# Split weights of the first layer: stored to device memory when first made, loaded by later token chunks

## The chip, the cores and the metric

The kernel runs on one core of one Trainium2 chip. The metric is device time in microseconds, the median of several executions. A core has five engines with an instruction stream each: PE (matrix products; its weight loads are listed as PEld), DVE (elementwise work), ACT (elementwise work with lookup functions), POOL (elementwise work, here mostly for splitting numbers and for rotary embedding) and SP, whose instructions here issue transfers. Each engine takes its instructions in the order in which they stand and waits where one needs a result from another engine.

## The reference

Two layers of a hybrid decoder with 1024 channels, over 16 learned meta tokens and 2048 input tokens (2064 rows). The first layer is what the change touches:

```
def swa_conv_mixer(h, pos, w_in, sinks, conv_w, conv_b, ln_g, ln_b, w_pw2, w_out):
    q, k, v, g_a, glu_in, g_b = _split(h @ w_in, AB_SPLITS)
    q, k = apply_rope(q, pos), apply_rope(k, pos)
    a = sliding_window_sink_attention(q, k, v, sinks) * silu(g_a)
    u = glu_in[..., :512] * sigmoid(glu_in[..., 512:])
    c = silu(layer_norm(causal_depthwise_conv(u, conv_w, conv_b), ln_g, ln_b))
    c = (c @ w_pw2) * silu(g_b)
    return concatenate([a, c], axis=-1) @ w_out
h = h + rms_norm(swa_conv_mixer(rms_norm(h, ...), ...), ...)
```

`w_in` is 1024 x 2816, `w_pw2` 512 x 512, the convolution has 31 taps. The second layer is stick-breaking attention with its own projections. Everything is float32.

## The kernel before

**Split numbers.** A matrix product in float32 accuracy is made of three products of rounded numbers (type float32r): a number x is split into a high part (x rounded) and a low part (x minus the high part), and `mm3` (L126 to L130) adds high x high, high x low and low x high into one PSUM bank. In the rows of the profile, `hTh` and `hTl` are the high and low parts of the normed input, `wh` and `wl` those of a weight block.

**Weights.** `weights` (L112 to L121) brings one block of 128 x 8 x 128 float32 (512 KB): SP loads it into `raw` (L118), ACT rounds it into `wh` (L119), POOL subtracts it into `wl` (L120). `raw`, `wh` and `wl` have two buffers each for the input projection. L118 is given a priority 60 places earlier than its place in the program, so that loads run ahead.

**Stages of the first layer.** The tokens are worked on in four chunks: 528 tokens (chunk 0, in two pieces of 272 and 256) and three of 512. `stage1` does the input projection of a chunk: 22 blocks of `w_in`, each by a call of `proj` (L277 to L287): one `weights`, then 24 matmuls of 512 columns (48 narrower ones in chunk 0), then a follow-up on ACT or DVE. The order is: two halves of the gated unit (`glu_b`, `glu_a`), key, value, queries, and eight gate blocks (`gate`, L360 to L370), whose results are stored by L369 (`gad`, `gbd`). Block `glu_a` also puts a convolution of 31 taps per channel group into a list; a tap is one DVE instruction over the chunk (L294), and `run_bg` gives out six of them after each projection. `rope` shuffles halves by four small transfers (L334) and does its arithmetic on DVE and POOL (L338 to L343).

`stage2` does the rest for a chunk, in 128-token blocks: sliding-window attention (`swa`: scores on PE L429, masking and maximum on DVE L430, exponentials on ACT L441, products L470) and the convolution branch (`cbranch`: layer norm, activation, and the second product in `pw` with `w_pw2`, two weight blocks per call by the same `weights`, once for each of eight groups of blocks). Stage 2 of a chunk is interleaved with stage 1 of the next, one step at a time, so both run at once from chunk 1 on. After chunk 3 come its stage 2, interleaved with the output projection (`po`), and then layer 1.

**What sets the order.** The program is written with tile pools, and a scheduler orders each engine's instructions from their dependencies, priorities and buffer turns. All transfers are issued by SP in one order.

So each of the 22 blocks of `w_in` is loaded, rounded and subtracted four times, once per chunk, and each of the two blocks of `w_pw2` eight times: 104 calls of `weights` in all.

Of the kernel before, what the change touches and what calls it, by code (L numbers as in the profile page):

```python
# [11 lines left out]
F32R = mybir.dt.float32r  # L12
# [6 lines left out]
P = 128  # L19
D = 1024  # L20
KB = D // P
# [16 lines left out]
WP = 60  # L38
# [14 lines left out]
def tok0(t):  # L53
    return 0 if t == 0 else NM + (t - 1) * P


def toks(t):
    return NM if t == 0 else P
# [20 lines left out]
class Trunk:  # L79
# [29 lines left out]
        self.nc.gpsimd.tensor_scalar(hi, src, 1.0, 0.0, ALU.mult, ALU.add)  # L109
        self.nc.vector.tensor_tensor(lo, src, hi, ALU.subtract)  # L110

    def weights(self, pool, src, rpool, tag):  # L112
        nc = self.nc
        raw = rpool.tile([P, KB, P], F32, tag=tag, name="raw", bufs=2 if tag == "raw" else 1)
        wh = pool.tile([P, KB, P], F32R, tag="wh", name="wh")
        wl = pool.tile([P, KB, P], F32R, tag="wl", name="wl")
        with self.tc.high_priority(offset=WP):
            self.wdma = nc.sync.dma_start(raw, src).ins  # L118
        nc.scalar.copy(wh, raw)  # L119
        nc.gpsimd.tensor_tensor(wl, raw, wh, ALU.subtract)  # L120
        return wh, wl  # L121

    def mv(self, out, src):
# [54 lines left out]
    def layer0(self, after=None):  # L178
        tc, nc, a = self.tc, self.nc, self.a
        HALO = CW - 1  # L180
        qd = self.dram("q0d", [P, 2, 4, T], F32R)
        kd = self.dram("k0d", [2, 2, HD, T], F32R)
# [6 lines left out]
        c0, w2, w3 = (self.pool(left, n, b, side="left") for n, b in (("c0", 1), ("w2", 2), ("w3", 3)))  # L189
# [5 lines left out]
        pww = self.pool(left, "pww", 2, side="left")  # L195
# [3 lines left out]
        s1c, s1, s3 = (self.pool(early, n, b, side="right") for n, b in (("s1c", 1), ("s1", 2), ("s3", 2)))  # L199
# [51 lines left out]
        def stage1(c):  # L251
# [23 lines left out]
            steps.append((0.0, start))  # L275

            def proj(m, evac):  # L277
                wh, wl = self.weights(pww, a["w_in0"][m], s1, "raw")
                turns = late[:]
                late.clear()  # L280
                for s0, sn in subs:
                    ps = self.bank(next(banks), "pj")
                    for k in range(KB):
                        self.mm3(ps[:, :sn], wh[:, k], wl[:, k], st["h"][:, k, s0 : s0 + sn], st["l"][:, k, s0 : s0 + sn], k == 0, k == KB - 1)
                    evac(ps[:, :sn], s0, sn)
                for f in turns:
                    f()  # L287
# [12 lines left out]
            def glu_b(j):  # L300
                sg = s1.tile([P, 528], F32, tag="sg", name="sg")
                st["sg"] = sg
                proj(14 + j, lambda ps, s0, sn: nc.scalar.activation(sg[:, s0 : s0 + sn], ps, AF.Sigmoid))
                run_bg(CB)

            def glu_a(j):
                sg = st["sg"]
                u = s1.tile([P, HALO + 528], F32, tag="u", name="u")
                y = s1.tile([P, 528], F32, tag="y", name="y")
                nc.gpsimd.tensor_scalar(u[:, :HALO], uh[:, j], 1.0, 0.0, ALU.mult, ALU.add)  # L310
                proj(10 + j, lambda ps, s0, sn: nc.vector.tensor_tensor(u[:, HALO + s0 : HALO + s0 + sn], ps, sg[:, s0 : s0 + sn], ALU.mult))
                nc.gpsimd.tensor_scalar(uh[:, j], u[:, TC : TC + HALO], 1.0, 0.0, ALU.mult, ALU.add)
                conv(j, u, y)
                run_bg(CB)
# [14 lines left out]
            def rope(m, put):  # L329
                qr = s1.tile([P, 528], F32, tag="qr", name="qr", bufs=3)  # L330
                qs = s1.tile([P, 528], F32, tag="qs", name="qs")
                proj(m, lambda ps, s0, sn: nc.scalar.copy(qr[:, s0 : s0 + sn], ps))
                for b in range(4):
                    nc.sync.dma_start(qs[b * 32 : b * 32 + 32, :TC], qr[(b ^ 1) * 32 : (b ^ 1) * 32 + 32, :TC])  # L334
                run_bg(CB)

                def turn():
                    nc.vector.tensor_tensor(qr[:, :TC], qr[:, :TC], st["ctab"][:, :TC], ALU.mult)  # L338
                    nc.gpsimd.tensor_tensor(qs[:, :TC], qs[:, :TC], st["stab"][:, :TC], ALU.mult)
                    nc.vector.tensor_tensor(qr[:, :TC], qr[:, :TC], qs[:, :TC], ALU.add)  # L340
                    hi, lo = qs[:, :TC].bitcast(F32R), qr[:, :TC].bitcast(F32R)
                    nc.gpsimd.tensor_scalar(hi, qr[:, :TC], 1.0, 0.0, ALU.mult, ALU.add)
                    nc.gpsimd.tensor_tensor(lo, qr[:, :TC], hi, ALU.subtract)  # L343
                    put(qs, qr)

                late.append(turn)
# [132 lines left out]
        def cbranch(ut):  # L479
            b0 = tok0(ut[0])  # L480
            N = sum(toks(t) for t in ut)
            S = {}

            def stats():
                yl = w2.tile([P, 4, 272], F32, tag="yl", name="yl", bufs=1)
                nc.sync.dma_start(yl[:, :, :N], yd[:, :, b0 : b0 + N].rearrange("r p t -> p r t"))
                mv = w2.tile([P, 3, 2], F32, tag="mv", name="mv")
                nc.vector.memset(mv, 1.0)
                S["yns"] = yns = []
                for i, t in enumerate(ut):  # L490
                    n, o = toks(t), tok0(t) - b0
                    pt = self.bank("pt", "pt_y")
                    for j in range(4):
                        nc.tensor.transpose(pt[:n, j * P : j * P + P], yl[:, j, o : o + n], self.ident)
                    st = w2.tile([P, 6], F32, tag="bst", name="bst")
                    nc.vector.bn_stats(st[:n], pt[:n])
                    nc.vector.bn_aggr(mv[:n, i], st[:n])
                    yn = w3.tile([P, 512], F32, tag="yn", name="yn")
                    nc.scalar.copy(yn[:n], pt[:n])
                    yns.append(yn)  # L500
                cr = w2.tile([P, 3], F32, tag="cr", name="cr")
                self.rsqrt(w2, cr, mv[:, :, 1], 1.0, LEPS, 3, nc.gpsimd)
                for i, t in enumerate(ut):
                    n = toks(t)
                    nc.vector.tensor_scalar(yns[i][:n], yns[i][:n], mv[:n, i, 0:1], cr[:n, i : i + 1], ALU.subtract, ALU.mult)

            def act():
                yns = S["yns"]
                S["ch"] = ch = w2.tile([P, 4, 272], F32R, tag="ch", name="ch", bufs=1)
                S["cl"] = cl = w2.tile([P, 4, 272], F32R, tag="cl", name="cl", bufs=1)  # L510
                for j in range(4):
                    pt = self.bank("pt", "pt_c")
                    for i, t in enumerate(ut):
                        n, o = toks(t), tok0(t) - b0
                        nc.tensor.transpose(pt[:, o : o + n], yns[i][:n, j * P : j * P + P], self.ident[:n, :n])
                    sg = w2.tile([P, 272], F32, tag="csg", name="csg")
                    tt = w2.tile([P, 272], F32, tag="ctt", name="ctt")
                    nc.scalar.activation(sg[:, :N], pt[:, :N], AF.Sigmoid, bias=cv[:, 2, j : j + 1], scale=cv[:, 1, j : j + 1])
                    nc.scalar.activation(tt[:, :N], pt[:, :N], AF.Identity, bias=cv[:, 2, j : j + 1], scale=cv[:, 1, j : j + 1])
                    nc.vector.tensor_tensor(tt[:, :N], tt[:, :N], sg[:, :N], ALU.mult)  # L520
                    nc.scalar.copy(ch[:, j, :N], tt[:, :N])
                    nc.vector.tensor_tensor(cl[:, j, :N], tt[:, :N], ch[:, j, :N], ALU.subtract)

            def pw():
                ch, cl = S["ch"], S["cl"]
                gb = w2.tile([P, 4, 272], F32, tag="gb", name="gb", bufs=1)
                nc.sync.dma_start(gb[:, :, :N], gbd[:, :, b0 : b0 + N].rearrange("r p t -> p r t"))
                for m in range(4):
                    if m % 2 == 0:
                        wh, wl = self.weights(pww, a["w_pw2"][m // 2], w2, "yl")  # L530
                    ps = self.bank("pj", "pw")
                    for k in range(4):
                        kk = 4 * (m % 2) + k
                        self.mm3(ps[:, :N], wh[:, kk], wl[:, kk], ch[:, k, :N], cl[:, k, :N], k == 0, k == 3)
                    tt = w2.tile([P, 272], F32, tag="ctt", name="mc")
                    nc.vector.tensor_tensor(tt[:, :N], ps[:, :N], gb[:, m, :N], ALU.mult)
                    nc.sync.dma_start(md[4 + m, :, b0 : b0 + N], tt[:, :N])

            return stats, act, pw
# [580 lines left out]
```

## Time and profile before

| | |
|---|---|
| median of three executions | 2995.03 us (2994.13 to 2998.02) |
| the profiled execution, its own time | 2996.4 us |
| its span, first to last instruction | 2994.7 us |
| PE, DVE, ACT, POOL busy | 92%, 79%, 51%, 50% |
| L120 `wl` on POOL, whole span | 104 instructions, 273.4 us |
| L119 `wh` on ACT, until 1000 us | 102 instructions, 106.9 us |
| L294 taps on DVE, whole span | 480 instructions, 515.4 us |
| moved by DMA | 395.77 MB, of which 270.21 MB read from and 116.97 MB written to device memory |

The profile is of one execution. A row of a group gives line, engine, operation, output and inputs, shape and count, then busy time and the mean of one, then the engine's idle time before it and whose result ended it. A row of waits reads "who <- for whom: total us, times, longest". Matmuls overlap, and their shown lengths are modelled; the distance from one start to the next tells their pace. The clock is the share of full speed that PE was granted.

### The profile page before, as it was taken

What the parts mean: (1) busy time and instruction counts of PE and PEld (TensorE: products, weight loads), DVE (VectorE), ACT (ScalarE), POOL (GpSimd) and SP (SyncE); (2) the same over time, 40 slices, a digit from 0 to 9 for tenths busy, and PEclk for the clock granted to TensorE, in tenths of its full rate; (3) what the DMA queues carried; (4) which work ended last, traced back from release to release, by engine and by line L of the source; (5) the groups of instructions that cost most, each with busy time, mean ns of one, the idle gap of its engine ahead of it and who ended that gap; (6) DMA issues with size and microseconds to landing.
All of it is one profiled execution on the core that took longest, in us unless ns stands there. A gap on an engine that the chain in (4) does not pass through costs nothing.

```text
span 2994.7 us, 49703 instructions
## 1 busy us (share of the span) xinstructions
PE 2761.3 (92%) x16110; PEld 2211.2 (74%) x16110; DVE 2358.1 (79%) x3656; ACT 1518.2 (51%) x3607; POOL 1483.4 (50%) x2580
## 2 busy tenths in 40 slices
PE   7788897887899999999999899999999999989998
PEld 6776676676668789888888677777777767766776
DVE  7989989989977683566667888788787888887874
ACT  4224343433455532455544566676676666755551
POOL 4645546455421122354445766565565566665430
PEclk9889898998999999999999999999999999999999
DMA  4445555455476566344445554234242332344322
GB/s 160 141 133 148 154 166 142 148 163 147 137 203 199 175 219 183 116 131 133 132 134 171 168 137 119 86 86 114 68 111 64 100 100 72 92 121 127 106 96 88
DMA packets 285556, 395.77 MB, mean 132 GB/s; under 512 B 44593, under 2 KB 198593, under 8 KB 282225
## 3 DMA queue, kind: packets, MB, share of 16 engines
q1 hardware_dynamic: 285296, 392.59, 44.4%
q8 instruction: 129, 2.11, 0.3%
q14 instruction: 131, 1.07, 0.1%
HBM read 270.21 MB, written 116.97 MB: 129 GB/s over the span
## 4 chain that ended last, share of the span: by engine, by line
PE 60%; DVE 21%; issue 6%; POOL 5%; ACT 4%; DMA 3%; SPq 1%; DVEq 0%; POOLq 0%; ACTq 0%
DVE y L294 11%; PE pj L128 8%; PE pj L129 8%; PE pj L130 8%; PE z L898 7%; PE av L944 7%; PE pt L930 7%; PE po L128 4%; PE po L130 4%; PE po L129 3%; DVE S L910 2%; ACT om L902 1%; DMA raw<-in_w_in 1%; DVE p L446 1%; ACT be L903 1%
## 5 line engine op out<-in xcount | busy, mean ns | idle before, releaser
L910 DVE TENSOR_TENSOR_SCAN S<-om,S 128x384 f32<-128x384 f32 (+5 forms) x768 | 744.2, 988 | 150.3 <-POOL om L906 67.7
L294 DVE SCALAR_TENSOR_TENSOR y<-u,cw,y 128x512 f32<-128x512 f32 (+1 forms) x480 | 515.4, 1079 | 7.3
L902 ACT ACTIVATE om<-z 128x384 f32<-128x384 f32 (+5 forms) x768 | 379.3, 512 | 209.5 <-PE z L898 135.2
L128 PE MATMUL pj<-th,wh 128*128 128x512 f32 (+2 forms) x1280 | 460.7, 360 | 8.0 <-POOL wh L109 4.5
L913 DVE TENSOR_TENSOR be<-be,S 128x384 f32<-128x384 f32 (+5 forms) x768 | 403.0, 549 | 72.7 <-ACT be L903 33.8
L130 PE MATMUL pj<-th,wl 128*128 128x512 f32 (+2 forms) x1280 | 452.4, 353 | 0.3 <-DVE wl L110 0.3
L129 PE MATMUL pj<-tl,wh 128*128 128x512 f32 (+2 forms) x1280 | 451.2, 352 | 0.0
L936 ACT COPY aT<-pt 128x512 f32<-128x512 f32 (+2 forms) x672 | 334.8, 505 | 201.2 <-PE pt L930 157.0
L898 PE MATMUL z<-kst,qt 128*128 128x384 f32 (+6 forms) x1536 | 396.4, 358 | 28.1 <-ACT be L903 26.9
L903 ACT ACTIVATE be<-z 128x384 f32<-128x384 f32 (+5 forms) x768 | 375.9, 506 | 76.5 <-PE pt L930 75.8
L930 PE MATMUL pt<-ident,be 128*128 128x128 f32 x2176 | 363.3, 281 | 24.3 <-ACT aT L936 9.7
L120 POOL TENSOR_TENSOR wl<-raw,wh 128x1024 fp32r<-128x1024 f32 x104 | 273.4, 2631 | 177.1 <-ACT wh L119 176.9
L912 POOL TENSOR_SCALAR carry<-S 128x1 f32<-128x1 f32 x512 | 265.8, 521 | 184.8 <-DVE S L910 160.3
L130 PE MATMUL pj<-hTh,wl 128*128 128x512 f32 (+2 forms) x880 | 321.7, 368 | 25.3 <-POOL wl L120 25.3
L930 PEld LDWEIGHTS pt<-ident,be 128*128 128x128 f32 x2176 | 252.7, 141 | 120.5 <-ACT aT L936 35.1
L128 PE MATMUL pj<-hTh,wh 128*128 128x512 f32 (+2 forms) x880 | 325.8, 371 | 12.3 <-DVE gt L366 6.4
L909 POOL TENSOR_SCALAR S<-carry 128x1 f32<-128x1 f32 x512 | 263.6, 517 | 136.6 <-DVE be L913 116.5
L129 PE MATMUL pj<-hTl,wh 128*128 128x512 f32 (+2 forms) x880 | 322.6, 367 | 1.3 <-DVE hTl L176 1.3
L898 PEld LDWEIGHTS z<-kst,qt 128*128 128x128 f32 x1536 | 249.0, 191 | 72.6 <-ACT be L903 51.9
L944 PE MATMUL av<-aT,vt 128*64 128x256 f32 (+1 forms) x2304 | 282.1, 381 | 4.6 <-DVE og L962 4.6
L128 PEld LDWEIGHTS pj<-th,wh 128*128 128x128 f32 x1280 | 241.8, 189 | 35.0 <-POOL wh L109 4.9
L130 PEld LDWEIGHTS pj<-th,wl 128*128 128x128 f32 x1280 | 240.9, 188 | 30.0 <-DVE wl L110 0.6
(177 smaller groups left out, 4817.4 us busy)
## 6 DMA issues: line engine op xcount, KB each, us to landing
raw<-in_w_in SPq DMA_DIRECT2D x164, 512.0 KB, 3.7
qt<-qhd SPq DMA_DIRECT2D x256, 64.0 KB, 2.6
qt<-qld SPq DMA_DIRECT2D x256, 64.0 KB, 2.4
kst<-khd SPq DMA_DIRECT2D x16, 516.0 KB, 7.8
kst<-kld SPq DMA_DIRECT2D x16, 516.0 KB, 10.0
qT<-q0d SPq DMA_DIRECT2D x32, 256.0 KB, 3.6
raw<-in_w_pw SPq DMA_DIRECT2D x16, 512.0 KB, 3.9
rawo<-in_w_out SPq DMA_DIRECT2D x16, 512.0 KB, 4.5
```

Source lines behind the costliest of these rows:

```text
L128: mm(out, sh, mh, start=first, stop=False)
L129: mm(out, sh, ml, start=False, stop=False)
L130: mm(out, sl, mh, start=False, stop=last)
L294: return lambda: nc.vector.scalar_tensor_tensor(y[:, :TC], u[:, w : w + TC], cw[:, j, w : w + 1], y[:, :TC], ALU.mult, ALU.add)
L898: nc.tensor.matmul(z[:, :n], S["q"][2 * h + i][:, x * P : x * P + P], S["k"][h][:, k0 : k0 + n], start=(i == 0), stop=(i == 1))
L902: nc.scalar.activation(om[:, :n], z[:, :n], AF.Sigmoid, scale=-0.125)
L903: nc.scalar.activation(be[:, :n], z[:, :n], AF.Sigmoid, scale=0.125)
L910: nc.vector.tensor_tensor_scan(P_[:, :n][:, ::-1], om[:, :n][:, ::-1], om[:, :n][:, ::-1], P_[:, n : n + 1], ALU.mult, ALU.bypass)
L913: nc.vector.tensor_tensor(be[:, :n], be[:, :n], P_[:, 1 : n + 1], ALU.mult)
L930: nc.tensor.transpose(pt[:, o : o + P], bes[h, x][:, mo + b * P : mo + b * P + P], self.ident)
L936: cps.append(nc.scalar.copy(aT[:, lo:hi], pt[:, lo:hi]))
L944: mi = nc.tensor.matmul(av[h * HD : h * HD + HD, qc0 + x0 : qc0 + 256], S["v"][:, b0 + b, h * HD : h * HD + HD], at, start=not S["started" ...
```

## The change

`weights` gets the name of a place in device memory. On the first call for a block it does what it did before and then stores `wh` and `wl` there (two stores of 512 KB, issued by SP). On every later call it loads both straight into `wh` and `wl` (two loads of 512 KB), without `raw`, the copy on ACT and the subtraction on POOL. The loads have the priority of the former load. Blocks of `w_in` are named by their number, so chunk 0 makes all 22 and chunks 1 to 3 load them (66 calls); the two blocks of `w_pw2` are made by the first group and loaded by the seven others (14 calls). That makes 24 first calls and 80 later ones.

```diff
-    def weights(self, pool, src, rpool, tag):
+    def weights(self, pool, src, rpool, tag, kept):
         nc = self.nc
+        if kept in self.drams:
+            wh = pool.tile([P, KB, P], F32R, tag="wh", name="wh")
+            wl = pool.tile([P, KB, P], F32R, tag="wl", name="wl")
+            with self.tc.high_priority(offset=WP):
+                for i, w in enumerate((wh, wl)):
+                    self.mv(w, self.drams[kept][:, i])
+            return wh, wl
+        kd = self.dram(kept, [P, 2, KB, P], F32R)
         raw = rpool.tile([P, KB, P], F32, tag=tag, name="raw", bufs=2 if tag == "raw" else 1)
         wh = pool.tile([P, KB, P], F32R, tag="wh", name="wh")
         wl = pool.tile([P, KB, P], F32R, tag="wl", name="wl")
...
         nc.scalar.copy(wh, raw)
         nc.gpsimd.tensor_tensor(wl, raw, wh, ALU.subtract)
+        for i, w in enumerate((wh, wl)):
+            self.mv(kd[:, i], w)
         return wh, wl
...
-                wh, wl = self.weights(pww, a["w_in0"][m], s1, "raw")
+                wh, wl = self.weights(pww, a["w_in0"][m], s1, "raw", f"wk{m}")
...
-                        wh, wl = self.weights(pww, a["w_pw2"][m // 2], w2, "yl")
+                        wh, wl = self.weights(pww, a["w_pw2"][m // 2], w2, "yl", f"wp{m // 2}")
```

In the changed program the line numbers after `weights` are larger by 10 (the taps stand at L304, the gate stores at L379); `mv` is at L134, and the copy and the subtraction at L127 and L128. Three places show how the order of instructions changes.

POOL, in chunk 1, where the rotary work (`qs`, `qr`) of its first blocks stands. Before:

```order
L120 TENSOR_TENSOR wl<-raw,wh 128x1024 x2
L447 TENSOR_SCALAR pmc<-p 128x128
L339 TENSOR_TENSOR qs<-qs,stab 128x512
L120 TENSOR_TENSOR wl<-raw,wh 128x1024
L339 TENSOR_TENSOR qs<-qs,stab 128x512
L342 TENSOR_SCALAR qs<-qr 128x512
L88 TENSOR_SCALAR rs_m<-ss 128x1
L343 TENSOR_TENSOR qr<-qr,qs 128x512
```

and in the changed program:

```order
L349 TENSOR_TENSOR qs<-qs,stab 128x512
L352 TENSOR_SCALAR qs<-qr 128x512
L353 TENSOR_TENSOR qr<-qr,qs 128x512
L349 TENSOR_TENSOR qs<-qs,stab 128x512
L352 TENSOR_SCALAR qs<-qr 128x512
L353 TENSOR_TENSOR qr<-qr,qs 128x512
L88 TENSOR_SCALAR rs_m<-ss 128x1
L457 TENSOR_SCALAR pmc<-p 128x128
```

The subtractions between the rotary steps are gone; the rest stands in a similar order.

SP, in chunk 1, at the gate blocks, whose order of blocks is 6, 7, 8, 17, 13, 9, 18. `gt` numbers tell the block: before, 2935 is block 6, 3003 block 7, 3076 block 8, and `raw` 3173, 3260 and 3344 are the weights of blocks 17, 13 and 9:

```order
L118 DMA raw_3173<-in_w_in0 128x1024
L369 DMA gad_82<-gt_2935 128x512
L118 DMA raw_3260<-in_w_in0 128x1024
L118 DMA raw_3702<-in_w_pw2 128x1024
L234 DMA xt_4962<-in_x 128x1024
L118 DMA raw_3344<-in_w_in0 128x1024
L369 DMA gad_82<-gt_3003 128x512
L369 DMA gad_82<-gt_3076 128x512
```

In the changed program the place in device memory carries the block's number (`wk8`, `wk17`), and `gt` 2977, 3043 and 3114 are blocks 6, 7 and 8:

```order
L134 DMA wh_3115<-wk8_1421 128x1024
L134 DMA wl_3116<-wk8_1421 128x1024
L379 DMA gad_82<-gt_2977 128x512
L134 DMA wh_3209<-wk17_1494 128x1024
L134 DMA wl_3210<-wk17_1494 128x1024
L379 DMA gad_82<-gt_3043 128x512
L244 DMA xt_4958<-in_x 128x1024
L134 DMA wh_3294<-wk13_1564 128x1024
L134 DMA wl_3295<-wk13_1564 128x1024
L379 DMA gad_82<-gt_3114 128x512
```

Ahead of the store of block 6 stood the load of block 17, three blocks on; now the last load ahead of it is that of block 8, two blocks on.

SP, in chunk 0, from its second weight block on, in the changed program; `wk14` and so on are now destinations:

```order
L134 DMA wk14_249<-wl_252 128x1024
L126 DMA raw_388<-in_w_in0 128x1024
L134 DMA wk10_313<-wh_315 128x1024
L134 DMA wk10_313<-wl_316 128x1024
L126 DMA raw_465<-in_w_in0 128x1024
L244 DMA xt_1391<-in_x 128x1024
L244 DMA xt_1707<-in_x 128x1024
L134 DMA wk4_387<-wh_389 128x1024
```

Each raw load stands behind the stores of the block before the last; before the change the loads of input tokens and raw weights followed one another there without stores. In layer 1 the instructions of all engines stand as before.

## The prediction

> **What bounds the kernel now.** I read the chain of waits first, then busy time in stretches, then single instructions. The first layer runs in stretches that end where the last `gbd` store of a token chunk is issued: chunk 0 until 209 us, chunk 1 until 408, chunk 2 until 633, chunk 3 until 839; then the rest of the layer until about 1130, then layer 1. The second line is the chain's shares by line; in the rows after it the columns are stretch, length, and busy time with instructions of PE, PEld, DVE, ACT and POOL, then granted clock, DMA share, GB/s.
>
> ```profile
> span 2994.7 us, 49703 instructions
> DVE y L294 11%; PE pj L128 8%; PE pj L129 8%; PE pj L130 8%; PE z L898 7%; PE av L944 7%; PE pt L930 7%; PE po L128 4%; PE po L130 4%; PE po L129 3%; DVE S L910 2%; ACT om L902 1%; DMA raw<-in_w_in 1%; DVE p L446 1%; ACT be L903 1%
> ...
> 0.00:209.00 209.00, 161.68 (x1163) 155.23 (x1163) 186.00 (x214) 63.86 (x110) 114.27 (x99) 0.94 0.44 138
> 209.00:408.00 199.00, 167.97 (x786) 131.78 (x785) 185.79 (x325) 81.41 (x183) 99.47 (x90) 0.92 0.54 154
> 408.00:633.00 225.00, 187.00 (x903) 148.43 (x901) 211.49 (x324) 90.80 (x185) 117.79 (x97) 0.91 0.50 146
> 633.00:839.00 206.00, 180.73 (x857) 143.55 (x857) 189.40 (x309) 82.11 (x169) 103.83 (x79) 0.92 0.52 153
> 839.00:1130.00 291.00, 279.46 (x1482) 226.12 (x1481) 213.04 (x536) 150.80 (x301) 50.05 (x65) 0.98 0.69 205
> ```
>
> Most of the change falls in the 630 us from 209 to 839 ("the stage" below): 66 of the 80 later weights are the first projection's, chunks 1 to 3. There DVE is busy 185.79 + 211.49 + 189.40 = 586.7 us (93%), PE 535.7 us (85%), and the chain of the whole span has the convolution's taps (L294) as its longest line, 11%. In the stretch after 839 PE is at 96%. So DVE sets the stage, with PE close behind.
>
> Why DVE is so full shows in single instructions: a tap alone, a tap beside the weight subtraction, all taps of the stage (min/median/max in ns), their busy time, and POOL's groups.
>
> ```profile
> 249.84 0.75 DVE L294 SCALAR_TENSOR_TENSOR y<-u,cw,y 128x512 f32<-128x512 f32 x1
> 256.90 2.58 POOL L120 TENSOR_TENSOR wl<-raw,wh 128x1024 fp32r<-128x1024 f32 x1 [0.89 <-ACT wh L119]
> 257.16 2.88 DVE L294 SCALAR_TENSOR_TENSOR y<-u,cw,y 128x512 f32<-128x512 f32 x1
> L294 DVE SCALAR_TENSOR_TENSOR y<-u,cw,y x366: 699/751/2964, 208.7 to 836.5; 128x512 f32<-128x512 f32 x180, 128x528 f32<-128x528 f32 x3
> 209.00:839.00 630.00, 384.23 (x366) 0.92 0.52 151
> L120 POOL TENSOR_TENSOR wl<-raw,wh 128x1024 fp32r<-128x1024 f32 x73 | 191.3, 2623 | 136.0 <-ACT wh L119 135.7
> L339 POOL TENSOR_TENSOR qs<-qs,stab 128x512 f32<-128x512 f32 x15 | 25.6, 1705 | 20.1 <-DMA qs<-qr 18.3 <-PE pj L130 1.0 <-PE s L429 0.8
> L343 POOL TENSOR_TENSOR qr<-qr,qs 128x512 fp32r<-128x512 f32 x15 | 24.4, 1628 | 1.1
> ```
>
> The tap at 249.84 takes 0.75 us. The one at 257.16 takes 2.88 us: it ends at about 260.0, just after the POOL subtraction that began at 256.90 ends at 259.5. A tap that meets POOL's two-input work stands still until that is done.
>
> **What the change removes: DVE's standstills.** 366 taps at the median 0.751 us would be 274.9 us; they take 384.23 us, so 109 us is standing still. Other DVE lines pay too: their means lie above their own quiet values.
>
> ```profile
> L446 DVE TENSOR_SCALAR p<-p,l 128x272 f32<-128x272 f32 x88 | 35.6, 474 | 0.0
> L446 DVE TENSOR_SCALAR p<-p,l x104: 216/351/2526, 218.1 to 808.1; 128x272 f32<-128x272 f32 x88, 16x16 f32<-16x16 f32 x8, 128x144 f32<-128x144 f32 x8
> L246 DVE SCALAR_TENSOR_TENSOR xs<-xt,rstd,gpre 128x1024 f32<-128x1024 f32 x6 | 14.0, 2336 | 3.8 <-POOL rstd L93 3.8
> L246 DVE SCALAR_TENSOR_TENSOR xs<-xp,rstd,gpre 128x1024 f32<-128x1024 f32 x4 | 4.9, 1274 | 0.0
> ```
>
> L446 pays 88 x (0.474 - 0.351) = 11 us, L246 6 x (2.336 - 1.274) = 6 us; with a few us for smaller lines I estimate 130 us. POOL's two-input work in the stage is 191.3 us of weights and 25.6 + 24.4 = 50.0 us of rotary; the weights' share is 79%. Of the stage's 73 subtractions two stay (the first makings of the second matrix fall there), so DVE is relieved of 130 x 0.79 x 71/73 = 100 us. Bounds: nothing, if the taps merely meet other waits, and 71 x 2.62 = 186 us, if each subtraction had cost its whole length.
>
> On that upper bound the Trainium skill has a rule: "SBUF — State Buffer", section "SBUF: two separate sides", says that DVE with two SBUF inputs and GpSimd take one shared port pair as a lock for a whole instruction, and that the loser is blocked entirely. The 2.88 us tap agrees; the average here, 100 us over 71, is 1.4 us, since DVE is not always at such an instruction. By the rule at its fullest the relief would be the 186 us, and the stage would go to PE's own limit, which is the second rival below.
>
> **How much of 100 us reaches the end.** PE is idle 630 - 535.7 = 94.3 us in the stage. Its waits there, each with total, count and longest:
>
> ```profile
> PE s L429 <- DVE mx L430: 47.6, 19, 6.0
> PE pw L128 <- DVE mc L536: 18.4, 4, 8.4
> PE s L429 <- DVE gt L366: 7.9, 3, 4.4
> PE pj L130 <- POOL wl L120: 6.0, 4, 2.8
> PE s L429 <- DVE hTl L176: 4.2, 1, 4.2
> PE pj L128 <- DVE mx L430: 2.6, 1, 2.6
> PE av L457 <- DVE mt L474: 2.5, 1, 2.5
> ```
>
> 83 us of them are for DVE. A DVE that is 100 us freer takes most of these away, and no more than these unless PE itself gets faster. It may: its clock is 0.92 in the stage and 0.98 where it hardly waits, and consecutive 512-column matmuls start 0.24 us apart at full clock:
>
> ```profile
> 252.26 0.40 PE L128 MATMUL pj<-hTh,wh 128*128 128x512 f32 x1
> 252.50 0.40 PE L129 MATMUL pj<-hTl,wh 128*128 128x512 f32 x1
> ...
> L128 PE MATMUL pj<-hTh,wh 128*128 128x512 f32 x520 | 216.1, 416 | 3.8 <-DVE mx L430 2.6 <-DVE mc L536 1.2
> ```
>
> By that, the projections' 3 x 520 = 1560 matmuls need 1560 x 0.235 = 367 us; the other 2546 - 1560 = 986 are about half as wide or less, 0.12 us each, 118 us: an estimate of 485 us for PE. DVE needs 586.7 - 100 = 487 us. Two engines with equal work, each filling the other's buffers, do not both run full; DVE's present 93% is with PE well below it. I take 89% of both: 486/0.89 = 546 us, **84 us less**. That is also the 83 us of PE's waits. Bounds of this term: 40 us (half passes on) and 130 us (a stage of 500 us).
>
> **What it adds: transfers in place of 3.7 us of engine work.** Before, a weight is ready one copy (ACT, 1.05 us) and one subtraction (2.62 us) after PE lets its buffer go, because the raw load has two tiles of its own and is there already. Afterwards two 512 KB loads start at that moment. The nearest rows:
>
> ```profile
> L119 ACT CAST wh<-raw 128x1024 fp32r<-128x1024 f32 x73 | 76.5, 1049 | 195.3 <-PE pj L129 97.7 <-issue 37.9 <-DMA raw<-in_w_pw 28.3
> L118 SPq DMA_DIRECT2D raw<-in_w_in x63: 328/372/743, 209.3 to 811.4; - x63
> DMA to landing us min/median/max: 3.1/3.9/8.5
> q1 hardware_dynamic: 285296, 392.59, 44.4%
> ...
> h<-bx SPq DMA_DIRECT2D x8, 512.0 KB, 4.1
> ```
>
> One load lands 3.9 us after its issue. The queue moved 392.59 MB in 44.4% of 2994.7 us, 3.39 us per MB, so 512 KB is 1.8 us of all 16 engines, and the second of the pair lands at about 0.4 + 3.9 + 1.4 = 5.7 us (an estimate; between 4 and 9, by 3.1 and 8.5 for one). With hand-offs it is 6 us against 4 now. The other buffer's projection, 24 x 0.235 = 5.6 us, and whatever scores and transposes stand between, run meanwhile: 546/66 = 8.3 us per projection. So these two microseconds are hidden, and I cost them at nothing; without that cover they are 66 x 2 = 132 us.
>
> DMA load: 71 more loads in the stage are 71 x 1.8 = 128 us on top of 0.52 x 630 = 328 us, together 456 of 546 us, a share of 0.83. Busier than any stretch above, but below the stage's length; it is part of why I don't take more than 84 us. ACT loses 71 x 1.05 = 75 us of work, but it is only 40% busy; what counts is that its waiting for PE (97.7 us at L119) no longer holds up copies queued behind it. I price that at nothing and keep it for the lower end.
>
> The wait now sits on SP, and SP is in order. What is queued behind a load that waits for PE are the rotary shuffles, the query and key loads and the gate stores; and a load can itself stand behind a gate store, which waits for DVE:
>
> ```profile
> SPq L118 <- POOL wl L120: 90.2, 27, 8.4
> SPq L369 <- DVE gt L366: 79.4, 16, 9.0
> ```
>
> SP already waits 90.2 us at the weights' loads; that wait changes its releaser. But the gate stores' 5 us each (79.4/16) was absorbed by loads three to four projections ahead; the order shows two ahead now.
>
> **Chunk 0** keeps all its splits and gets 44 stores, 44 x 1.8 = 79 us of DMA on 0.44 x 209 = 92 us, a share of 0.82. Each raw load now stands behind the two stores, but it waited for the same subtraction before, and the weight it brings is needed a projection later (209/22 = 9.5 us). The four-piece rotary shuffles may land later. A store of the same size (`h<-bx`, above) lands in 4.1 us, so none holds a buffer until its next use. The loss is bounded below by nothing, above by 22 x 0.7 us (two issues of 0.37) = 16 us of SP time laid bare. I take **5 us lost**, nearer to nothing since all 22 raw loads run ahead. **After 839** seven splits go where PE is at 96%: 7 x 1.4 = 10 us of DVE relief of which little shows, and the order of PE's work changes; I take **3 us gained**, within 8 either way. Layer 1's order is the same and counts as zero.
>
> **Sum**: 84 - 5 + 3 = 82 us less. The profiled execution took 2996.4 us (its span 2994.7, 1.7 around it), so 2914 us; that execution is 1.4 us above the median of the three, 2995.03, so the prediction is 2913 us.
>
> **Rivals.**
> 1. PE and DVE get in each other's way: only half of the relief passes on, 42 us or less. For it: both would need 486 us, and clock 0.5 stretches come after PE's waits. Against: 83 of 94 us of PE's idle time are for DVE. 2996.4 - 42 - 1.4 + 2 = 2955 us.
> 2. All the relief and ACT's and POOL's freed queues: the stage goes to 500 us, PE's 485 with little waiting. 2995 - 130 + 2 = 2867 us. For it: subtractions that had cost their whole length (186 us); against: 97% on PE beside an equally loaded DVE, which no stretch of this layer up to 839 shows.
> 3. Slower: the weights' loads come late through SP's order. Mechanism: load behind a gate store or a shuffle that waits for DVE, PE without weight. With 5 us late on half of 66 weights it is 165 us on PE against 84 gained: 2995 + 81 + 2 = 3078 us. It decides from 84/66 = 1.3 us late on every weight, beyond what the projection in between hides. For it: two instead of four tiles of lead; against: 8.3 us per projection against 6 us of transfer.
> 4. The path alternates between engines so that relief is eaten by later loads: 2995 us, no change.
>
> **How the numbers follow.** Forecast (2875 to 2940) 0.60; rival 1 0.17; rival 2 0.11; rival 3 0.07; rival 4 0.05. Faster by over 0.2% (6 us, about what a measurement of this kernel can tell from no change): 0.88; within 0.2%: 0.05; slower: 0.07. The range takes in rival 1 and most of rival 2: 2868 to 2962 us.
>
> **What would show it.** In the changed profile: 24 subtractions in all; the taps' mean between 209 us and the end of chunk 3 near 0.8 us instead of 1.05, the median unchanged; that stage at 530 to 565 us; 25 MB more written and 42 MB more read. PE's waits for DVE should shrink. New rows "PE pj <- DMA wh" or "wl" over 30 us would mean rival 3 is at work; a stage under 515 us rival 2. The prediction is wrong if the taps quicken and the stage does not, or if chunk 0 grows by more than 15 us.

## The result, and the profile after

The changed kernel takes 2947.06 us (median of four runs, 2944.07 to 2951.05) against 2994.58 us of the kernel before (four runs): a ratio of 0.9842, 95% interval 0.9824 to 0.986, 47.5 us less. The forecast was 82 us less (2913 us), likeliest between 2875 and 2940 us, in a range from 2868 to 2962 us. The result lies in the range, and 7 us above the likeliest band.

Stretches of the changed kernel, cut at the same marks as before (the last `gbd` store of each chunk; the columns are those of the prediction's first table):

```profile
0.00:202.00 202.00, 157.82 (x1145) 152.60 (x1145) 177.34 (x221) 59.27 (x105) 110.86 (x96) 0.94 0.76 257
202.00:385.00 183.00, 170.78 (x815) 132.80 (x815) 154.99 (x322) 66.28 (x167) 49.92 (x71) 0.96 0.79 234
385.00:587.00 202.00, 179.24 (x869) 141.93 (x868) 158.62 (x317) 65.56 (x156) 39.31 (x69) 0.94 0.78 230
587.00:790.00 203.00, 179.79 (x863) 141.91 (x861) 157.03 (x309) 61.46 (x146) 35.07 (x55) 0.94 0.78 227
```

Its page's lines on traffic and on the chain that ended last (shares by line):

```profile
DMA packets 303987, 462.88 MB, mean 157 GB/s; under 512 B 46640, under 2 KB 200640, under 8 KB 300656
HBM read 312.16 MB, written 142.14 MB: 154 GB/s over the span
...
PE pj L140 11%; PE pj L138 11%; PE pj L139 11%; PE z L908 7%; PE pt L940 7%; PE av L954 6%; PE po L138 4%; PE po L139 4%; PE po L140 4%; DMA wl<-wk 2%; DVE S L920 2%; DVE y L304 2%; ACT om L912 1%; DMA raw<-in_w_in 1%; ACT be L913 1%
```

The stage (chunks 1 to 3) went from 630 to 588 us, 42 less. Chunk 0 went from 209 to 202 us. From the last `gbd` store to layer 1's first matmul it is 273 us in both. The spans of the two profiled executions (2994.7 and 2942.2 us) differ by 52.5 us; the 3 to 4 us that this leaves over stand in layer 1, whose instructions are the same in both. The chain has turned over: the taps fell from 11% to 2%, the projections' matmuls rose from 24% to 33%, and a transfer that was not there before, `wl<-wk`, stands on it with 2%. Traffic grew by 67 MB, 42 of them reads and 25 writes, as the change says.

The taps of the stage by their line (min/median/max in ns):

```profile
L304 DVE SCALAR_TENSOR_TENSOR y<-u,cw,y x364: 698/752/2750, 202.2 to 787.6; 128x512 f32<-128x512 f32 x180, 128x528 f32<-128x528 f32 x2
```

Their busy time as a stretch of its own:

```profile
202.00:790.00 588.00, 296.63 (x364) 0.95 0.78 230
```

And the page's rows of the later loads (count, size, median us from issue to landing):

```profile
wh<-wk SPq DMA_DIRECT2D x66, 512.0 KB, 4.8
wl<-wk SPq DMA_DIRECT2D x66, 512.0 KB, 6.0
```

The median tap is as long as before (752 ns), the sum fell from 384.2 to 296.6 us: standing still is what went. DVE as a whole is busy 154.99 + 158.62 + 157.03 = 470.6 us in the stage, 116 less than before. Only 42 of these 116 us reached the end of the stage. In the trace before, 74 of the stage's taps take over 1 us: 50 of them lie across a weight subtraction and hold 92 of the 110 us by which the taps together exceed their median, 21 lie across rotary work and hold 18. In the trace after, 23 us are left, 18 of them beside rotary work. What PE waits for in the stage now (total, times, longest):

```profile
PE pj L140 <- DMA wl<-wk: 14.6, 10, 6.5
PE pj L138 <- DMA wh<-wk: 13.6, 7, 3.4
PE s L439 <- DVE mx L440: 11.6, 6, 3.7
PE pw L138 <- DVE mc L546: 3.7, 2, 2.2
PE pt_v L364 <- ACT vt L366: 3.5, 1, 3.5
PE pj L138 <- DVE mx L440: 3.5, 2, 3.1
PE pj L138 <- DVE y L304: 2.4, 1, 2.4
PE pj L138 <- DVE mv L507: 1.3, 1, 1.3
```

Waits for DVE fell from 83 to 23 us. Waits for weights, 6 us before, are now 28 us. That is 60 gained and 22 given back; PE's busy time fell by 6 us (535.7 to 529.8). Together 44 us, which is the stage's gain within 2 us.

Why PE waits for weights: in the trace I matched each of the 80 later weights with the last matmul that used its buffers before. From the start of that matmul until both parts have landed it is 7.3 us in the median, 8.5 in the mean and 12.8 at the ninth tenth; in 25 of 80 cases PE's first matmul stands less than 0.5 us behind the landing of the second part, or ahead of it, so that PE stops for `wl`. SP issues the first load 0.2 us after the buffer is free in the median, 1.3 in the mean, and up to 17 us late.

### The profile page after: what moved, and what is told of

It is laid out like the page before. It is cut to its first block, busy times and chain, and to the rows that moved or that the text cites. A ratio compares the mean times of both kernels' runs of the same rounds, so it can differ in the third digit from the quotient of the medians.

```text
span 2942.2 us, 49705 instructions
## 1 busy us (share of the span) xinstructions
PE 2749.7 (93%) x16110; PEld 2200.3 (75%) x16110; DVE 2230.0 (76%) x3656; ACT 1445.5 (49%) x3529; POOL 1263.4 (43%) x2500
## 4 chain that ended last, share of the span: by engine, by line
PE 69%; DMA 9%; DVE 8%; issue 5%; POOL 4%; ACT 4%; SPq 2%; DVEq 0%; POOLq 0%; ACTq 0%
PE pj L140 11%; PE pj L138 11%; PE pj L139 11%; PE z L908 7%; PE pt L940 7%; PE av L954 6%; PE po L138 4%; PE po L139 4%; PE po L140 4%; DMA wl<-wk 2%; DVE S L920 2%; DVE y L304 2%; ACT om L912 1%; DMA raw<-in_w_in 1%; ACT be L913 1%
## 5 line engine op out<-in xcount | busy, mean ns | idle before, releaser
L304 DVE SCALAR_TENSOR_TENSOR y<-u,cw,y 128x512 f32<-128x512 f32 (+1 forms) x480 | 425.0, 886 | 9.4
L139 PEld LDWEIGHTS pj<-tl,wh 128*128 128x128 f32 x1280 | 241.4, 189 | 25.7 <-issue 0.8
```

Of the source, the lines that this page charges most:

```text
L139: mm(out, sh, ml, start=False, stop=False)
L304: return lambda: nc.vector.scalar_tensor_tensor(y[:, :TC], u[:, w : w + TC], cw[:, j, w : w + 1], y[:, :TC], ALU.mult, ALU.add)
```

## The experiments

Three theories on the 35 us that are missing. **A, lead**: a load can only start when PE lets a buffer go, one projection before it is needed. **B, pace**: PE can't do more than it does, 530 busy of 588 us. **C, traffic**: at a DMA share of 0.78 transfers land late. Beside them stands rival 3 of the prediction, SP's order.

**A third pair of buffers.** Every third later block of the input projection goes into the two tiles that held raw weights in chunk 0, so no memory is added and the bytes are the same.

```diff
         if kept in self.drams:
-            wh = pool.tile([P, KB, P], F32R, tag="wh", name="wh")
-            wl = pool.tile([P, KB, P], F32R, tag="wl", name="wl")
+            self.turn = getattr(self, "turn", -1) + (tag == "raw")
+            if tag == "raw" and self.turn % 3 == 2:
+                wh, wl = (rpool.tile([P, KB, P], F32R, tag="raw", name=n, bufs=2) for n in ("wh", "wl"))
+            else:
+                wh = pool.tile([P, KB, P], F32R, tag="wh", name="wh")
+                wl = pool.tile([P, KB, P], F32R, tag="wl", name="wl")
```

> The changed kernel with a third pair of buffers for the loaded weights of the input projection: every third later block goes into the two tiles that the raw weights used in chunk 0, so a load can start one projection earlier; nothing else differs, the same bytes move. Theory A (lead: a weight is ready 7.3 us, median, after PE lets its buffer go, and in 25 of 80 cases PE uses it within 0.5 us of landing): PE's waits for weight transfers in the stretch of chunks 1 to 3 fall from 28 us to under 8, the stretch from 588 us to 550-565, the kernel from 2947 to 2920-2930 us. Theory B (pace: PE busy 530 of 588 us is all that it can do): within 6 us of 2947. Theory C (traffic: a DMA share of 0.78 makes all transfers late): the time from free buffer to landing stays or grows, the waits move to other transfers, and the kernel stays at 2940 us or more.

Measured: 2900.34 us, ratio to before 0.9686 (0.967 to 0.9703), 47 us under the changed kernel: the gain doubled. Between the two profiled executions (2944.07 and 2906.35 us) it is 38 us, 36 of them in the stage. The stage as a stretch:

```profile
202.00:754.00 552.00, 517.60 (x2535) 410.91 (x2535) 465.44 (x945) 195.22 (x470) 135.06 (x194) 0.96 0.80 246
```

PE's waits in it:

```profile
PE pw L142 <- DVE mc L550: 6.8, 2, 3.8
PE pt_c L529 <- ACT vt L370: 5.6, 4, 2.4
...
PE pj L142 <- DMA wh<-wk: 3.2, 6, 0.9
PE pj L144 <- DMA wl<-wk: 2.8, 5, 1.1
```

The waits for weights are 6.0 us, no single one over 1.1. The stage takes 552 us at a DMA share of 0.80, a little higher than before, so it was not the share that held it at 588. This is what theory A says; B falls, and so does C as the main cause. PE's own busy time fell by 12 us as well, with its clock at 0.96. The stage lies in A's range, but the kernel came out 20 us under it.

**No loads at all.** Later calls take the pair of tiles that is there, without loading it. The 160 later transfers are left out and the products use one block's weights for others, so that only the time is of use.

```diff
         if kept in self.drams:
-            ...
-            return wh, wl
+            return self.last
...
+        self.last = wh, wl
         return wh, wl
```

> The changed kernel with the 80 later loads left out: later calls take the pair of tiles that is there, so the output is not the reference's. It shows what the stage costs without splits and without loads. Theories A and C: 2905-2920 us, the stretch of chunks 1 to 3 at 540-560 us. Theory B: 2940 us or more, with PE busy about 530 us in that stretch. Between A and C: if the run with three buffers comes within 6 us of this one, lead was all; what is left between the two is traffic.

Measured: 2876.46 us, 0.9609 (0.9594 to 0.9623). Its stage:

```profile
202.00:724.00 522.00, 499.44 (x2519) 401.22 (x2518) 459.79 (x947) 200.03 (x473) 136.32 (x194) 0.98 0.42 115
```

522 us is what both engines can do when weights cost nothing: PE is busy 96% of it, DVE 88%. So PE and DVE don't hold each other at 588 us. The stage is 66 us shorter than the changed kernel's: PE is idle 36 us less and busy 30 us less, at a clock of 0.98 instead of 0.95. Of the 71 us between the changed kernel and this one, the third pair brings back 47; 24 remain. The time is lower than any theory expected (the lowest range began at 2905 us).

**Half of the bytes, three buffers.** `wh` is loaded as in the first run, `wl` is not: later calls take the `wl` that is there. Half of the later transfers are left out (42 MB less is read) and the low parts are those of another block, so that again only the time is of use.

```diff
-                for i, w in enumerate((wh, wl)):
-                    self.mv(w, self.drams[kept][:, i])
-            return wh, wl
+                self.mv(wh, self.drams[kept][:, 0])
+            return wh, self.last
```

> Three buffers for wh, loaded as before, but wl isn't loaded: later calls take the wl tile that is there, so the output is not the reference's; 42 MB less is read. Between the run with three pairs (2900 us) and the one without loads (2876 us) lie 24 us. Theory C for this rest (bytes: a DMA share of 0.80 against 0.42): about half of it goes, 2884-2892 us. Rival (a rest of waiting for transfers to land, whatever their size, and of SP's order): 2896-2902 us.

Measured: 2881.78 us, 0.9626 (0.9612 to 0.964), 18.6 us of the 24. Its stage:

```profile
202.00:732.00 530.00, 509.14 (x2537) 404.47 (x2538) 464.29 (x940) 195.75 (x471) 131.55 (x194) 0.98 0.62 184
```

530 us at a share of 0.62. So most of the rest goes with the second load, a little more than theory C expected (2884 to 2892 us). It is not proved that bytes are its cause: half the transfers are gone as well, SP issues fewer of them, and `wh` had a little more lead than in the first run, because the raw tiles give it two places.

**The loads issued by ACT.** Two pairs, the same bytes, another queue.

```diff
-                    self.mv(w, self.drams[kept][:, i])
+                    nc.scalar.dma_start(w.bitcast(F32), self.drams[kept][:, i].bitcast(F32))
```

> The changed kernel with the 160 later loads issued by ACT instead of SP; two pairs of buffers, the same bytes. Theory A (lead): a load still starts only when PE lets a buffer go, so 2935-2955 us. Rival 3 of the prediction (SP's order: loads stand behind stores that wait for DVE, and other transfers behind loads that wait for PE; a load was issued 1.3 us after its buffer was free in the mean, up to 17): 2925 us or less. If ACT's own work is held up by waiting for PE, as it was at L119 before the change: 2960 us or more.

Measured: 2930.76 us, 0.9791 (0.9777 to 0.9806), 16 us under the changed kernel. This lies between the two ranges, under that of the lead alone (2935 to 2955 us) and above that of SP's order as the main cause (2925 us or less). Matched as above, a weight is ready 7.3 us after its buffer is free in the mean, against 8.5, and issued 0.5 us after it in the mean, against 1.3. PE's waits in the stage:

```profile
PE s L439 <- DVE mx L440: 11.3, 7, 3.7
PE pj L140 <- DMA wl<-wk: 9.2, 10, 2.6
...
PE pj L138 <- DMA wh<-wk: 4.6, 5, 1.5
```

Waits for weights halve, from 28 to 14 us. SP's order was a part of the lateness, and what the other queue brings is about a third of what the third pair brings. The loss that a held-up ACT would have given (2960 us or more) did not come.

**Stores alone.** The kernel before, with the 48 stores and without any later load.

```diff
+        seen = kept in self.drams
+        kd = self.dram(kept, [P, 2, KB, P], F32R)
...
+        if not seen:
+            for i, w in enumerate((wh, wl)):
+                self.mv(kd[:, i], w)
```

> The kernel before, with the 48 stores alone: wh and wl are stored when first made, and never loaded; all 104 splits stay. My prediction's term: 5 us lost in chunk 0 (between nothing and 16), so 2995 to 3011 us, likeliest 3000; chunk 0 ends at 209 to 225 us. Rival (chunk 0 ended 7 us earlier in the changed kernel because stores change the order in its favour): 2985-2990 us.

Measured: 2996.84 us, 1.0013 (1.0003 to 1.0022), 3.3 us more. Chunk 0:

```profile
0.00:206.00 206.00, 161.56 (x1163) 154.95 (x1163) 181.83 (x217) 63.09 (x110) 116.72 (x98) 0.95 0.73 252
```

It ends at 206 us instead of 209, though its DMA share rose from 0.44 to 0.73: chunk 0 itself lost nothing. The loss came later, for the stage took 637 us instead of 630. The stores are nearly free. That chunk 0 ends at 202 us in the changed kernel goes along with fewer subtractions in it (25 began before its end in the kernel before, 24 here, 22 in the changed kernel); that these are the cause is not shown.

**The subtraction on DVE.** The kernel before with one word changed; nothing is stored or loaded anew.

```diff
-        nc.gpsimd.tensor_tensor(wl, raw, wh, ALU.subtract)
+        nc.vector.tensor_tensor(wl, raw, wh, ALU.subtract)
```

> The kernel before, with the subtraction that makes wl on DVE instead of POOL; no stores, no loads from the kept place. A DVE subtraction of this size takes 1.21 us (L110), and DVE lost about 1.6 us to each of POOL's (116 us over 71). If DVE's standstills behind POOL's subtraction are what the time before was made of: 104 x 0.4 = 40 us less work on DVE, and the kernel at 2960-2975 us. Rival (the subtraction now stands in DVE's order behind taps, wl comes late, and PE waits for it instead): 2995 us or more.

Measured: 2918.13 us, 0.975 (0.9735 to 0.9764): 75 us under the kernel before and 29 under the changed one. It is 42 us under the range that was expected (2960 to 2975 us): the sign was right, the size far too small. Its subtractions (min/median/max in ns):

```profile
L120 DVE TENSOR_TENSOR wl<-raw,wh x104: 1169/1218/2315, 13.3 to 950.3; 128x1024 fp32r<-128x1024 f32 x104
```

Its first two stretches, chunk 0 and the stage:

```profile
0.00:180.00 180.00, 152.20 (x1153) 147.05 (x1154) 150.81 (x221) 60.90 (x107) 52.76 (x73) 0.98 0.51 160
180.00:746.00 566.00, 524.80 (x2535) 415.31 (x2534) 527.75 (x1016) 262.00 (x542) 155.05 (x193) 0.95 0.57 167
```

PE's waits for weights in the stage:

```profile
PE pj L130 <- DVE wl L120: 9.0, 7, 2.5
PE pj L128 <- ACT wh L119: 8.1, 6, 3.7
```

DVE has 104 instructions more and is busy less, 2286.2 us against 2358.1. The pages' lines, before and in this run:

```profile
PE 2761.3 (92%) x16110; PEld 2211.2 (74%) x16110; DVE 2358.1 (79%) x3656; ACT 1518.2 (51%) x3607; POOL 1483.4 (50%) x2580
PE 2738.6 (94%) x16110; PEld 2194.2 (75%) x16110; DVE 2286.2 (78%) x3760; ACT 1524.6 (52%) x3611; POOL 1239.8 (42%) x2476
```

It loses 1.22 us per subtraction that it does itself and lost more to each of POOL's. DVE's relief of 72 us and the kernel's gain of 75 are not one and the same, though: at the end of chunk 3 this run is 93 us ahead (29 in chunk 0, 64 in the stage), and from there to layer 1's first matmul it takes 294 us instead of 273. Two waits of PE in that part make up most of the loss; where they come from I did not take apart:

```profile
PE s L429 <- DMA kT<-k0d: 11.9, 1, 11.9
PE pt_m L453 <- issue: 8.6, 1, 8.6
```

The run changes one more thing: a subtraction takes 1.22 us instead of 2.62, so each weight is ready sooner. In chunk 0 PE's waits for it show this, before and in this run:

```profile
PE pj L130 <- POOL wl L120: 19.3, 8, 5.8
PE pj L130 <- DVE wl L120: 7.9, 7, 1.8
```

So up to 11 of chunk 0's 29 us can be the sooner weight and not DVE's relief. In the stage, where the same wait was 6.0 us before and is 9.0 here, that rival falls. A weight still comes by a copy and a subtraction, with its raw load done before, and PE waits 17 us for weights in the stage, where the changed kernel waits 28.

**Both together.** Three pairs of buffers, and the 24 subtractions that are left on DVE.

> The run with three pairs of buffers (2900 us), and the 24 subtractions that are left on DVE instead of POOL. If DVE's standstills set chunk 0 as they set the later chunks before the change, chunk 0 shortens from 202 us towards the 180 us that it took with all subtractions on DVE, and the kernel takes 2875-2885 us. Rival (chunk 0 is held by something else once stores stand in SP's order): within 8 us of 2900.

Measured: 2882.39 us, 0.9622 (0.9606 to 0.9638). This is 18 us under three pairs alone, and as expected. Chunk 0's last `gbd` store is issued at 175 us, not at 202:

```profile
0.00:175.00 175.00, 148.17 (x1143) 143.44 (x1143) 146.65 (x222) 58.87 (x105) 56.23 (x73) 0.98 0.86 297
```

DVE is busy 147 us in it instead of 177. With nothing left out, the kernel is 65 us under the changed one. Issuing its later loads from ACT as well:

> Three pairs of buffers, the 24 subtractions on DVE (2882 us so far), and the later loads issued by ACT instead of SP. With two pairs, the other queue was worth 16 us (2947 to 2931). If SP's order still delays transfers with a third pair: 2865-2876 us. If a load that starts one projection earlier hides that delay: within 6 us of 2882. If ACT now waits for buffers where it should empty PSUM banks: 2890 us or more.

Measured: 2879.91 us, 0.962 (0.9604 to 0.9636), 2.5 us from the run before it, which the spread of either covers. With a third pair no cost of SP's order can be seen.

## Why the prediction was right, and where its size was off

- **DVE's standstills were the cost**: right. Forecast 100 us of relief in the stage, measured 116; the median tap unchanged, the mean 296.63/364 = 0.81 us. Of the 110 us by which the taps had exceeded their median, 92 lay across weight subtractions, 1.8 us for each of the 50 taps. The Trainium skill ("SBUF — State Buffer", section "SBUF: two separate sides") states that a DVE instruction with two SBUF inputs and a GpSimd one that reads SBUF lock each other out of a shared port pair for a whole instruction. The traces agree with a lock that is met often, not always: 71 subtractions less freed DVE of 116 us, 1.6 us each, where a whole subtraction takes 2.62.
- **How much reaches the end**: the forecast took 84 us, stage at 546 us, with the loads at no cost. The engines could do more: without loads the stage is 522 us, so "89% of both" was cautious by 24 us. The sum behind it was off as well, since PE's 485 us were reached by no run; PE was busy 529.8 us in the changed kernel and 499.4 without loads. The 83 us of PE's waits for DVE fell by 60.
- **The term that was mis-sized is the added transfers**, "these two microseconds are hidden, and I cost them at nothing". They cost 66 us in the stage (588 against 522 without loads) and 71 in the kernel. Of these the third pair takes back 36 and 47, so that much hung on the lead. Two things were off. The delay from free buffer to weight was put at 6 us and is 7.3 in the median and 8.5 in the mean: the second of a pair lands 6.0 us after its issue, not 5.3, at a share of 0.78, and SP adds 1.3. And the cover was taken as an average, 8.3 us per projection. Projections with little PE work in between have 5.6 us, and a tenth of the loads takes over 12.8 us. A lead of one projection has no room for such a spread; before, the raw load's own two tiles gave room, though no run takes them away to show it. The bound named for it, 0 to 132 us, held the cost; the value taken was its end. Nor did the waits alone make it up: of the 66 us, 30 are PE's own busy time, at a clock of 0.95 against 0.98.
- **Where the number fell** is in part luck. The two errors have opposite signs, 24 us of caution and 66 us of loads, and leave the stage 42 us above the forecast's 546. The sign that was named for it, a stage of 530 to 565 us, did not come. The range held the result because its upper end had been set to take in rival 1, whose mechanism the runs do not bear out.
- **The DMA share** was forecast at 0.83 and is 0.78, over a longer stage. What is left of its cost is at most the 24 us between three pairs and no loads.
- **Chunk 0** was forecast to lose 5 us and gained 7; with the stores alone it gained 3, and the kernel lost 3.3 behind it. **After 839**, 3 us were forecast, and none came up to layer 1's first matmul.
- **Rivals.** Rival 1 named nearly the stage's gain (42 us) but not its cause: without loads DVE's busy time is 127 us less than before (586.7 to 459.8) and the stage is 108 us shorter, so PE and DVE do not stop each other at half of the relief. Rival 2's 2867 us is near where the kernel would be with weights at no cost (2876), but its stage of 500 us was not reached (522). Rival 3's mechanism is at work at a smaller price: 28 us of waits. The other queue leaves 14 of them and the third pair 6, so SP's order and the short lead overlap and their shares can't be added. Its point of decision, 1.3 us on every weight, was not reached: 28 us over 66 weights is 0.4.

## What to carry to other kernels

Where DVE sets the time, compare the mean with the median of its commonest instruction. Here the difference, times the count, was 110 us, and nearly all of it stood beside POOL's two-input work; moving that work onto DVE itself may be the cheaper cure, as it was here against the change with two pairs (2918 against 2947 us). When arithmetic is replaced by a load, count the lead again from the moment at which the buffer is free, not from the middle of the pipeline: here the raw tiles that became idle were exactly the third pair that the loads needed, and it doubled the gain. A cover should be checked against the long loads and the short projections, not their averages.

## What the runs showed of the hardware

A subtraction of 128 x 1024 numbers takes POOL 2.62 us and DVE 1.22; over the kernel DVE was 72 us less busy with 104 of them added, so each of POOL's had cost DVE 72/104 + 1.22 = 1.9 us, more than the 1.6 that I had expected from the stage (116/71). Storing 25 MB more, at a DMA share in chunk 0 of 0.73 instead of 0.44, cost the kernel 3.3 us. PE's busy time is not fixed: for nearly the same matmuls of the stage (2546, 2535 and 2519 recorded) it was 535.7 us before, 517.6 with three pairs and 499.4 without loads, as the granted clock rose from 0.92 to 0.96 and 0.98. The traces' clock records show where the difference lies: PE had half the clock for 105 us of the stage before, 61 in the changed kernel, 41 with three pairs and 20 without loads, and each such stretch began behind 3.4 us in which PE had been idle for at least 1.6 us. So a wait of PE can cost more than its own length.
